# One order for the upper and lower passes in all four feed-forward halves, and another set of PSUM banks for their first block

## The chip, the cores and the metric

One core of a Trainium2 chip runs the whole program. The metric is the device time of one execution in microseconds; the median of the runs is given, and a profiled execution of its own shows where the time goes. TensorE (PE) multiplies, ScalarE (ACT) and VectorE (DVE) prepare its operands and read its results out of PSUM, SyncE (SP) issues the loads, and GpSimd (POOL) does little here.

## The reference

Two layers work on x of 256 tokens x 1024. What matters here are the two SwiGLU half steps of each layer, four in the program:

```
def swiglu(h, w_in, w_out):
    gate, up = jnp.split(h @ w_in, 2, axis=-1)
    return (jax.nn.silu(gate) * up) @ w_out

for i in range(DEPTH):                                    # DEPTH = 2, D_FF = 2816
    x = x + 0.5 * swiglu(rms_norm(x, norm_ffn1[i]), ffn1_w_in[i], ffn1_w_out[i])
    ...                                                   # attention, x = x + o @ w_o[i]
    x = x + 0.5 * swiglu(rms_norm(x, norm_ffn2[i]), ffn2_w_in[i], ffn2_w_out[i])
    ...                                                   # x = x + gate * (p[i] @ w_ple_proj[i])
```

## The kernel before

Every fp32 operand is split into an upper part and a lower part that PE takes as fp32r. For the weights, ACT writes the upper part `whi` (L236, L238) and DVE the lower part `wlo` (L243, L245), eight tiles ahead of PE at most. A product is upper x upper, upper x lower and lower x upper.

A half step (`ffn`) works on eleven blocks of 256 hidden columns. The **first block** has the tokens as its rows (`unit_cols`), one bank for each half of the tokens: 48 matmuls of 512 columns. Its result goes through Silu on ACT (L655) and a product on DVE (L661), and is turned by four PE transposes (`h_T`). In the first half step these two banks are of the kind `acc`; in the other three they are of the kind `mm`. The **other ten blocks** have the hidden columns as their rows (`columns`): four banks (two `mm`, one `tp`, one `op`) collect four chunks of weights. A chunk has eight pairs (k, n), n being the bank. A pair has an **upper pass** (`whi` against both parts of x, 512 columns) and a **lower pass** (`wlo` against the upper part of x, 256 columns). `COLUMN_GROUPS` says how many upper passes stand in a row ahead of their lower passes: 1 in the first half step, 2 in the second, 4 in the third, 8 in the fourth. After each column block come 24 or 18 matmuls of the output's product (`out_unit`, a **run** below) for an earlier block; they collect in the four `acc` banks. After the last block a run of 66 ends the half step.

The order on each engine is fixed when the program is built, by a model of the engines' times (`Pace`): helpers are put at the place at which the model finds their inputs ready and their bank free. The banks are four `acc`, two `mm`, one `tp` and one `op`; each kind is handed out in turn. At the end of a half step and of the attention the four `acc` banks are read into x by DVE (the attention's reading is L1130).

Of the kernel before, what the change touches and what calls it, by code (L numbers as in the profile page):

```python
# [108 lines left out]

COLUMN_GROUPS = (1, 2, 4, 8)


class Pace:
# [182 lines left out]
def encoder(ctx: ExitStack, tc, ins, out):  # L298
# [14 lines left out]
    pace = Pace()  # L313
# [6 lines left out]
    def can(kind):  # L320
        return slots[kind][turn[kind]] <= pace.now

    def take(kind, *tiles):
        assert can(kind), kind
        k = turn[kind]
        slots[kind][k] = 1e9
        turn[kind] = (k + 1) % len(slots[kind])
        for t in tiles:
            owner[id(t)] = (kind, k, t)
        return tiles[0] if len(tiles) == 1 else tiles  # L330
# [6 lines left out]
    def bank(kind):  # L337
        pool = {"acc": ps_acc, "mm": ps_mm}.get(kind, ps_tp)
        return take(kind, pool.tile([P, 512], F32, tag=kind, name=kind))
# [34 lines left out]
    def add_ffn(i, n, name):  # L374
        w_in, w_out = ins[name + "_in"][i], ins[name + "_out"][i]
        a, b = {}, {}
        for j in range(NFB):
            a[j] = add_cols(w_in[j], 2 * FB, n, i, uses=1 if j else 2)
            for m, kc, t in OUT_BEHIND.get(j, ()):
                if t == 0:  # L380
                    b[m, kc] = add_rows(w_out[2 * m + kc])
        for m, kc in OUT_LEFT:
            b[m, kc] = add_rows(w_out[2 * m + kc])
        return a, b

    plan = []
    for i in range(DEPTH):
        d = {"ffn1": add_ffn(i, 0, "ffn1")}
# [11 lines left out]
    def mm(ps, lhsT, rhs, start, stop, ready=0.0):  # L400
        nc.tensor.matmul(ps, lhsT=lhsT, rhs=rhs, start=start, stop=stop)  # L401
        pace.pe(0.0125 + rhs.shape[-1] / 2400, ready)
# [6 lines left out]
    def unit_cols(ps, a, t, ids, c, cw, kks=None):  # L409

        nk = 1024 // cw
        pace.until(lambda: all(a.cell[t][k].get("lo") for k in range(c * nk, c * nk + nk)))
        kks = kks or range(nk)
        wh, wl = W.get(ids[c])
        for kk in kks:
            k = c * nk + kk
            s = slice(kk * cw, (kk + 1) * cw)
            mm3(ps[:, :cw], a.hi[t][:, k, :], a.lo[t][:, k, :], wh[:, s], wl[:, s], k == 0, k == KD - 1,
                max(W.when[ids[c]], a.cell[t][k]["lo"]))
            if kk == nk - 1:  # L420
                W.used(ids[c])
            pace.check()
# [210 lines left out]
        pace.act(1500, pace.now)  # L633


    def ffn(a, ids, stage, first=False):

# [1 line left out]
        acc, hT, hs, made = [], {}, {}, {}  # L641
# [9 lines left out]
        def evac(t, ps, ts, done=None):  # L651
            pace.until(lambda: can("sq") and can("L") and a.has_r[t])
            s_t = scratch("sq")
            s = s_t[:, :FB]
            nc.scalar.activation(s, ps[:, :FB], AF.Silu, scale=a.r[t])  # L655
            t1 = pace.act(FB, max(done or pace.done(), a.has_r[t]), scale=True)
            if not hs:
                hs[0] = tile_L()

            def prod():  # L660
                nc.vector.tensor_tensor(out=hs[0][:, t, :], in0=ps[:, FB:], in1=s, op=ALU.mult)  # L661
                t2 = pace.dve(FB, t1)
                give(s_t)
                give(ps, t2)
                if ts:
                    with_bank("acc", t2 + 1.5, lambda: h_T(ts, t2))
            pace.at(t1, prod, "dve", 1)

        def first_evac(t, ps):
            if a.has_r[t]:  # L670
                evac(t, ps, [0, 1] if t else [], pace.now)
            else:
                pace.at(pace.now + 0.1, lambda: first_evac(t, ps))
# [34 lines left out]
        def columns(j):  # L708

            kinds = ("mm", "mm", "tp", "op")  # L710
            pace.until(lambda: all(max(slots[kind]) <= pace.now for kind in kinds))
            banks = [bank(kind) for kind in kinds]
            for c in range(4):
                ks = (2 * c, 2 * c + 1)
                pace.until(lambda: all(a.cell[t][k].get("lo") for t in range(2) for k in ks))
                wh, wl = W.get(ids_in[j][c])
                r = max(W.when[ids_in[j][c]], *(a.cell[t][k]["lo"] for t in range(2) for k in ks))
                every = [(k, n) for k in ks for n in range(4)]
                step = COLUMN_GROUPS[stage]
                for g in range(0, 8, step):  # L720
                    for lower in range(2):
                        for k, n in every[g:g + step]:
                            x2 = xhl[:, k, :, :].rearrange("p u q -> p (u q)")
                            o = slice(512 * (k % 2) + P * n, 512 * (k % 2) + P * (n + 1))
                            if lower:
                                mm(banks[n][:, S:], wl[:, o], x2[:, :S], False, k == KD - 1)
                            else:
                                mm(banks[n], wh[:, o], x2, k == 0, False, r)
                            pace.check()
                W.used(ids_in[j][c])  # L730
                pace.check()
            for kc in range(2):
                product(j, kc, banks[kc], banks[2 + kc])

        def product(j, kc, g_ps, u_ps):
            pace.until(lambda: can("sq") and "r" in has)
            gu = scratch("sq")
            g, u = gu[:, :S], gu[:, S:]
            p0 = pace.done()

            def gate():
                nc.scalar.copy(g, g_ps[:, :S])  # L742
                t1 = pace.act(S, p0)
                nc.scalar.copy(u, u_ps[:, :S])
                t2 = pace.act(S, p0)
                pace.at(t1, lambda: gate_sum(t1), "dve", 0)
                pace.at(t2, lambda: other_sum(t2), "dve", 1)

            def gate_sum(t1):
                nc.vector.tensor_tensor(out=g, in0=g_ps[:, S:], in1=g, op=ALU.add)  # L750
                give(g_ps, pace.dve(S, t1))
                nc.vector.tensor_tensor(out=g, in0=g, in1=rms_b, op=ALU.mult)
                t3 = pace.dve(S, has["r"])
                pace.at(t3, lambda: act(t3), "act", 1)

            def other_sum(t2):
                nc.vector.tensor_tensor(out=u, in0=u_ps[:, S:], in1=u, op=ALU.add)  # L757
                give(u_ps, pace.dve(S, t2))

            def act(t1):  # L760
                nc.scalar.activation(g, g, AF.Silu)
                t2 = pace.act(S, t1, sbuf=True)
                pace.at(t2, lambda: prod(t2), "dve", 1)

            def prod(t2):
                nc.vector.tensor_tensor(out=u, in0=u, in1=g, op=ALU.mult)
                t3 = pace.dve(S, t2)
                split(t3)

            def split(t3):  # L770
                if j not in hT and not can("pt"):
                    pace.at(pace.now + 0.1, lambda: split(t3))
                    return
                hh, hl = slot(j)
                made[j, kc] = parts(hh[:, kc, :], hl[:, kc, :], u, S, ready=t3, then=lambda end: give(gu))
            pace.at(p0, gate, "act", 1)
# [22 lines left out]
        ps = []  # L799
        pace.at(pace.now, lambda: spread(0))  # L800
        if first:
            ps = [bank("acc") for t in range(2)]
            for k in range(KD):
                for t in range(2):
                    unit_cols(ps[t], a, t, ids_in[0], k // 2, 512, [k % 2])
                    if k == KD - 1:
                        first_evac(t, ps[t])
        else:
            for t in range(2):
                pace.until(lambda: can("mm"))  # L810
                ps.append(bank("mm"))
                for c in range(4):
                    unit_cols(ps[t], a, t, ids_in[0], c, 512)
                evac(t, ps[t], [0, 1] if t else [])
        for j in range(1, NFB):
            columns(j)
            for unit in OUT_BEHIND[j]:
                out_unit(*unit)
# [391 lines left out]
    a = first_acts()  # L1210
# [2 lines left out]
    table(AF.Silu)  # L1213
    for i in range(DEPTH):
        d = plan[i]
        a = ffn(a, d["ffn1"], 2 * i, first=(i == 0))
        a, ple = mixers(i, a, d)
        a = ffn(a, d["ffn2"], 2 * i + 1)
        a = gate(a, d["gate"], ple, final=(i == DEPTH - 1))


# [14 lines left out]
```

## Time and profile before

| | us |
|---|---|
| median of 3 runs | 1037.63 |
| the runs | 1037.04 to 1039.37 |
| profiled execution | 1036.9 |
| its span on the core | 1035.1 |
| PE busy | 1021.1 (99%) |
| DVE busy | 767.5 (74%) |
| ACT busy | 687.1 (66%) |

The span is the time from the first to the last instruction of the program; the profiled execution's own time has 1.8 us around it. PE's records overlap: a matmul of 512 columns is shown with some 0.39 us, but the next starts some 0.23 us after it. So the pitch (start to start) is read, not the length. The four half steps lie at about 5 to 196, 311 to 498, 520 to 708 and 823 to 1009 us.

### The profile page before, as it was taken

What the parts mean: (1) busy time and instruction counts of PE and PEld (TensorE: products, weight loads), DVE (VectorE), ACT (ScalarE), POOL (GpSimd) and SP (SyncE); (2) the same over time, 40 slices, a digit from 0 to 9 for tenths busy, and PEclk for the clock granted to TensorE, in tenths of its full rate; (3) what the DMA queues carried; (4) which work ended last, traced back from release to release, by engine and by line L of the source; (5) the groups of instructions that cost most, each with busy time, mean ns of one, the idle gap of its engine ahead of it and who ended that gap; (6) DMA issues with size and microseconds to landing.
All of it is one profiled execution on the core that took longest, in us unless ns stands there. A gap on an engine that the chain in (4) does not pass through costs nothing.

```text
span 1035.1 us, 15614 instructions
## 1 busy us (share of the span) xinstructions
PE 1021.1 (99%) x5466; PEld 872.1 (84%) x5466; DVE 767.5 (74%) x1578; ACT 687.1 (66%) x1438; POOL 34.6 (3%) x38
## 2 busy tenths in 40 slices
PE   8999999999999999999999999999999999999998
PEld 7888888879887888888888888888888888888887
DVE  6686875888896757857887478578898876678575
ACT  8875754678886646746876467467779875467463
POOL 0000000120100000000000000001110000000000
PEclk9999999999999999999999999999999999999999
DMA  8664754455455546645664457444654466366361
GB/s 301 213 211 155 268 177 145 161 188 177 149 169 197 162 131 210 225 155 182 217 201 163 154 171 257 163 133 173 214 158 148 143 218 215 99 234 226 103 208 62
DMA packets 55911, 187.30 MB, mean 181 GB/s; under 512 B 6502, under 2 KB 10854, under 8 KB 55832
## 3 DMA queue, kind: packets, MB, share of 16 engines
q1 hardware_dynamic: 55832, 186.30, 54.3%
q8 instruction: 43, 0.70, 0.3%
q14 instruction: 36, 0.29, 0.1%
HBM read 185.19 MB, written 1.08 MB: 180 GB/s over the span
## 4 chain that ended last, share of the span: by engine, by line
PE 89%; DVE 5%; ACT 2%; DMA 2%; issue 1%; POOL 0%; SPq 0%; ACTq 0%
PE acc L401 34%; PE mm L401 28%; PE op L401 12%; PE tp L401 10%; PE tp L438 2%; DVE wlo L245 2%; DMA wraw<-in_ffn_in_dram 1%; DVE wlo L243 1%; DVE hss L862 1%; DMA wraw<-in_qkv_dram 1%; PE op L438 1%; ACT whi L238 1%; PE acc L438 0%; POOL hrs L866 0%; ACT kah L458 0%
## 5 line engine op out<-in xcount | busy, mean ns | idle before, releaser
L245 DVE SCALAR_TENSOR_TENSOR wlo<-wraw,gains,whi 128x512 fp32r<-128x512 f32 (+1 forms) x464 | 318.9, 738 | 54.5 <-ACT whi L238 52.9
L238 ACT ACTIVATE whi<-wraw,gains 128x512 fp32r<-128x512 f32 (+1 forms) x464 | 301.4, 707 | 70.0 <-DMA wraw<-in_ffn_in_dram 41.2
L401 PE MATMUL mm<-xhl,whi 128*128 128x512 f32 x640 | 211.7, 396 | 3.8 <-DVE L L661 3.5
L243 DVE TENSOR_TENSOR wlo<-wraw,whi 128x512 fp32r<-128x512 f32 x216 | 140.3, 686 | 29.8 <-ACT whi L236 24.5
L236 ACT CAST whi<-wraw 128x512 fp32r<-128x512 f32 x216 | 124.2, 617 | 56.5 <-PE op L401 29.3
L401 PE MATMUL mm<-xhl,wlo 128*128 128x256 f32 x640 | 140.5, 281 | 0.0
L401 PE MATMUL acc<-whi,pth 128*128 128x512 f32 x352 | 137.8, 392 | 0.0
L401 PE MATMUL acc<-whi,ptl 128*128 128x512 f32 x352 | 137.4, 390 | 0.0
L401 PE MATMUL acc<-wlo,pth 128*128 128x512 f32 x352 | 137.4, 390 | 0.0
L401 PEld LDWEIGHTS mm<-xhl,wlo 128*128 128x128 f32 x640 | 117.8, 189 | 17.0
L401 PE MATMUL tp<-xhl,whi 128*128 128x512 f32 x320 | 126.1, 394 | 0.2 <-DVE sq L757 0.2
L401 PE MATMUL op<-xhl,whi 128*128 128x512 f32 x320 | 126.3, 395 | 0.0
L401 PEld LDWEIGHTS mm<-xhl,whi 128*128 128x128 f32 x640 | 108.5, 189 | 19.3 <-DVE L L661 4.8
L750 DVE TENSOR_TENSOR sq<-mm,sq 128x256 f32<-128x256 f32 x80 | 33.7, 422 | 113.2 <-ACT sq L742 112.4
L401 PE MATMUL mm<-whi,xhl 128*128 128x512 f32 (+1 forms) x304 | 100.5, 391 | 0.0
L401 PE MATMUL tp<-xhl,wlo 128*128 128x256 f32 x320 | 89.7, 280 | 0.0
L401 PE MATMUL op<-xhl,wlo 128*128 128x256 f32 x320 | 89.4, 280 | 0.0
L742 ACT COPY sq<-mm 128x256 f32<-128x256 f32 x80 | 30.2, 377 | 88.2 <-PE mm L401 88.2
L401 PE MATMUL acc<-whi,xhl 128*128 128x512 f32 (+1 forms) x288 | 83.1, 363 | 1.0 <-ACT whi L238 1.0
L401 PEld LDWEIGHTS acc<-whi,ptl 128*128 128x128 f32 x352 | 66.1, 188 | 14.3
L401 PEld LDWEIGHTS acc<-whi,pth 128*128 128x128 f32 x352 | 66.1, 188 | 12.9
L401 PEld LDWEIGHTS acc<-wlo,pth 128*128 128x128 f32 x352 | 66.1, 188 | 12.4
(155 smaller groups left out, 1576.5 us busy)
## 6 DMA issues: line engine op xcount, KB each, us to landing
wraw<-in_ffn_in_dram SPq DMA_DIRECT2D x172, 512.0 KB, 4.5
wraw<-in_ffn_out_dram SPq DMA_DIRECT2D x88, 512.0 KB, 4.8
wraw<-in_qkv_dram SPq DMA_DIRECT2D x36, 512.0 KB, 3.5
wraw<-in_wo_dram SPq DMA_DIRECT2D x16, 512.0 KB, 3.5
wraw<-in_gate_dram SPq DMA_DIRECT2D x16, 512.0 KB, 4.5
bias<-bias_d SPq DMA_DIRECT2D x32, 192.0 KB, 4.0
wraw<-in_ffn_in_dram SPq DMA_DIRECT2D x8, 256.0 KB, 5.5
wraw<-in_ple_dram SPq DMA_DIRECT2D x4, 512.0 KB, 5.0
```

Source lines behind the costliest of these rows:

```text
L236: nc.scalar.copy(hi[:, a:b], raw[:, a:b])
L238: nc.scalar.activation(hi[:, a:b], raw[:, a:b], AF.Copy, scale=g)
L243: nc.vector.tensor_tensor(out=lo[:, a:b], in0=raw[:, a:b], in1=hi[:, a:b].bitcast(F32), op=ALU.subtract)
L245: nc.vector.scalar_tensor_tensor(out=lo[:, a:b], in0=raw[:, a:b], scalar=g, in1=hi[:, a:b].bitcast(F32), op0=ALU.mult, op1=ALU.subtract)
L401: nc.tensor.matmul(ps, lhsT=lhsT, rhs=rhs, start=start, stop=stop)
L438: nc.tensor.transpose(tp[:, n * P:(n + 1) * P], src, ident)
L742: nc.scalar.copy(g, g_ps[:, :S])
L750: nc.vector.tensor_tensor(out=g, in0=g_ps[:, S:], in1=g, op=ALU.add)
L862: nc.vector.tensor_reduce(out=ss[:, :nh], in_=sq[:, :w].rearrange("p (h d) -> p h d", d=HD), axis=AX.X, op=ALU.add)
```

## The change

```
-COLUMN_GROUPS = (1, 2, 4, 8)
+COLUMN_GROUP = 8
...
-    def ffn(a, ids, stage, first=False):
+    def ffn(a, ids, first=False):
...
-                step = COLUMN_GROUPS[stage]
+                step = COLUMN_GROUP
                 for g in range(0, 8, step):
                     for lower in range(2):
                         for k, n in every[g:g + step]:
...
         else:
             for t in range(2):
-                pace.until(lambda: can("mm"))
-                ps.append(bank("mm"))
+                pace.until(lambda: can("acc"))
+                ps.append(bank("acc"))
                 for c in range(4):
                     unit_cols(ps[t], a, t, ids_in[0], c, 512)
                 evac(t, ps[t], [0, 1] if t else [])
```

All half steps now have eight upper passes in a row and then eight lower ones, as the fourth had before. The two banks of the first block are `acc` in all four.

On PE, at the start of the first column block of the first half step (about 17.8 us), upper and lower passes alternated before:

```order
L401 MATMUL mm<-xhl,whi 128x512
L401 MATMUL mm<-xhl,wlo 128x256
L401 MATMUL mm<-xhl,whi 128x512
L401 MATMUL mm<-xhl,wlo 128x256
L401 MATMUL tp<-xhl,whi 128x512
L401 MATMUL tp<-xhl,wlo 128x256
L401 MATMUL op<-xhl,whi 128x512
L401 MATMUL op<-xhl,wlo 128x256
```

Now the block starts with:

```order
L401 MATMUL mm<-xhl,whi 128x512 x2
L401 MATMUL tp<-xhl,whi 128x512
L401 MATMUL op<-xhl,whi 128x512
L401 MATMUL mm<-xhl,whi 128x512 x2
L401 MATMUL tp<-xhl,whi 128x512
L401 MATMUL op<-xhl,whi 128x512
```

The fourth bank was first written by the seventh matmul; now the first four matmuls write all four banks.

On PE, at the end of the second half step's first block and the start of its first column block (about 321 us), this stood before:

```order
L401 MATMUL mm<-wlo,xhl 128x512
L401 MATMUL mm<-whi,xhl 128x512
L401 MATMUL mm<-xhl,whi 128x512 x2
L401 MATMUL mm<-xhl,wlo 128x256 x2
L401 MATMUL tp<-xhl,whi 128x512
L401 MATMUL op<-xhl,whi 128x512
L401 MATMUL tp<-xhl,wlo 128x256
L401 MATMUL op<-xhl,wlo 128x256
L401 MATMUL mm<-xhl,whi 128x512
L438 MATMUL acc<-ident,L 128x128 x4
```

This stands there now:

```order
L401 MATMUL acc<-wlo,xhl 128x512
L401 MATMUL acc<-whi,xhl 128x512
L401 MATMUL mm<-xhl,whi 128x512 x2
L401 MATMUL tp<-xhl,whi 128x512
L401 MATMUL op<-xhl,whi 128x512
L401 MATMUL mm<-xhl,whi 128x512 x2
L401 MATMUL tp<-xhl,whi 128x512
L401 MATMUL op<-xhl,whi 128x512
L401 MATMUL mm<-xhl,wlo 128x256 x2
L401 MATMUL tp<-xhl,wlo 128x256
L401 MATMUL op<-xhl,wlo 128x256
```

The matmuls of the first block write `acc` where they wrote `mm`, and so the two `mm` banks that the column block takes are no longer those that the first block has just filled. The four transposes of `h_T` (the last row of before) stand behind 20 passes of the column block, where they stood behind 9; in the third half step behind 16 instead of 9, in the fourth behind 17 instead of 7.

On ACT in the second half step, the split of the turned first block (L458, `pth`) stood behind three splits of weights:

```order
L655 ACTIVATE sq<-mm,r_3463 128x256
L238 ACTIVATE whi<-wraw,gains 128x512 x3
L458 CAST pth<-acc 128x512
L238 ACTIVATE whi<-wraw,gains 128x512 x4
```

Now it stands behind five:

```order
L655 ACTIVATE sq<-acc,r_3463 128x256
L238 ACTIVATE whi<-wraw,gains 128x512 x5
L458 CAST pth<-acc 128x512
L238 ACTIVATE whi<-wraw,gains 128x512 x2
```

DVE's lower parts move with it, and in the third half step both engines have one weight split more ahead of it. Nothing else changes its place on ACT, DVE, POOL or SP, and on PE everything outside the column passes and these transposes keeps its order.

## Rows read from the trace of the kernel before

**Rows 1.** The page: the clock that TensorE was granted, in 40 slices of the span.

```profile
PEclk9999999999999999999999999999999999999999
```

**Rows 2.** Waits of PE: engine, line, releaser: us in total, times, longest.

```profile
PE mm L401 <- DVE L L661: 3.5, 3, 1.6
```

**Rows 3.** Timeline of PE, second half step: start, length, instruction, [idle before <-releaser].

```profile
321.29 0.39 PE L401 MATMUL mm<-whi,xhl 128*128 128x512 f32 x1
321.51 0.39 PE L401 MATMUL mm<-xhl,whi 128*128 128x512 f32 x1
323.52 0.50 PE L401 MATMUL mm<-xhl,whi 128*128 128x512 f32 x1 [1.62 <-DVE L L661]
323.85 0.40 PE L401 MATMUL mm<-xhl,wlo 128*128 128x256 f32 x2
```

**Rows 4.** The same view at the same place of the third and fourth half steps.

```profile
531.73 0.39 PE L401 MATMUL mm<-xhl,whi 128*128 128x512 f32 x1
533.00 0.50 PE L401 MATMUL mm<-xhl,whi 128*128 128x512 f32 x1 [0.88 <-DVE L L661]
...
833.02 0.39 PE L401 MATMUL mm<-xhl,whi 128*128 128x512 f32 x1
834.43 0.50 PE L401 MATMUL mm<-xhl,whi 128*128 128x512 f32 x1 [1.01 <-DVE L L661]
```

**Rows 5.** Chain that ended last: start, length, piece. Runs of the output's product.

```profile
81.12 5.47 PE acc L401 x24
...
179.13 10.95 PE acc L401 x48
...
335.15 5.45 PE acc L401 x24
...
480.35 10.90 PE acc L401 x48
...
544.67 5.49 PE acc L401 x24
...
690.77 10.94 PE acc L401 x48
...
846.09 5.47 PE acc L401 x24
...
943.05 5.47 PE acc L401 x24
...
991.53 8.64 PE acc L401 x38
```

**Rows 6.** Timeline of PE, first half step (two rows), then fourth (two rows).

```profile
119.70 0.40 PE L401 MATMUL op<-xhl,whi 128*128 128x512 f32 x1
...
121.11 0.40 PE L401 MATMUL op<-xhl,whi 128*128 128x512 f32 x1
...
934.50 0.63 PE L401 MATMUL mm<-xhl,whi 128*128 128x512 f32 x2
...
937.30 0.63 PE L401 MATMUL mm<-xhl,whi 128*128 128x512 f32 x2
```

**Rows 7.** Timeline of PE, first half step, the fourth column block's start.

```profile
68.86 0.50 PE L401 MATMUL mm<-xhl,whi 128*128 128x512 f32 x1
...
70.90 0.40 PE L401 MATMUL op<-xhl,whi 128*128 128x512 f32 x1
```

**Rows 8.** Chain that ended last, ahead of that block.

```profile
59.53 5.34 DMA wraw<-in_ffn_in_dram
...
65.73 2.75 DVE wlo L245 x4
```

**Rows 9.** Timelines of DVE and PE, second half step: last bank read, next column block.

```profile
371.64 0.41 DVE L757 TENSOR_TENSOR sq<-op,sq 128x256 f32<-128x256 f32 x1
...
372.25 0.62 PE L401 MATMUL mm<-xhl,whi 128*128 128x512 f32 x2
```

**Rows 10.** Timeline of DVE ahead of the second half step: the reading of `acc`.

```profile
309.89 1.28 DVE L1130 TENSOR_TENSOR x_sb<-acc,x_sb 128x512 f32<-128x512 f32 x2
```

More of the change, by code (lines that the diff above doesn't have):

```diff
@@ L108 @@
 OUT_LEFT = [(j, kc) for j in range(NFB - 2, NFB) for kc in range(2)]
-COLUMN_GROUPS = (1, 2, 4, 8)
+COLUMN_GROUP = 8
 class Pace:
@@ L633, in table, with ffn @@
         pace.act(1500, pace.now)
-    def ffn(a, ids, stage, first=False):
+    def ffn(a, ids, first=False):
         ids_in, ids_out = ids
@@ L718, in columns @@
                 every = [(k, n) for k in ks for n in range(4)]
-                step = COLUMN_GROUPS[stage]
+                step = COLUMN_GROUP
                 for g in range(0, 8, step):
@@ L809, in ffn @@
             for t in range(2):
-                pace.until(lambda: can("mm"))
-                ps.append(bank("mm"))
+                pace.until(lambda: can("acc"))
+                ps.append(bank("acc"))
                 for c in range(4):
@@ L1215, in encoder @@
         d = plan[i]
-        a = ffn(a, d["ffn1"], 2 * i, first=(i == 0))
+        a = ffn(a, d["ffn1"], first=(i == 0))
         a, ple = mixers(i, a, d)
-        a = ffn(a, d["ffn2"], 2 * i + 1)
+        a = ffn(a, d["ffn2"])
         a = gate(a, d["gate"], ple, final=(i == DEPTH - 1))
```

## The prediction

> **What bounds the kernel now.** I read the page first, then the waits of PE, then the chain that ended last, and last the timelines around the places that the change touches. The page has PE busy in every slice, and the clock granted is full in all 40 [rows 1], which is the 2.4 GHz level: there is no clock to win or lose here, and time comes only from PE's pitch or from gaps between its matmuls. The list of waits has one entry over 3 us, three waits for the product of the first block [rows 2]. The timeline shows one of them: an upper pass into the first mm bank starts at 321.51, the next one, into the second mm bank, at 323.52, when DVE has read that bank out (L661) [rows 3]. The chain of the four half steps is nearly all PE in its alternation of column blocks and runs, so a pitch that is shorter there shortens the program.
>
> **The first block into acc.** The second mm bank holds the second half of the tokens, whose last matmul ends the first block. Silu and the product must pass before the column block can write there. With acc the two mm banks are long free. The usual pitch of a 512-column matmul is 0.22 to 0.23 us [rows 3], so the gaps lose 2.01 - 0.23 = 1.78 us in the second half step, 1.27 - 0.23 = 1.04 in the third and 1.41 - 0.23 = 1.18 in the fourth [rows 3, 4]: 4.0 in all. The matmul after such a gap has a pitch of 0.33 instead of 0.23 [rows 3]; I take that 0.1 as part of the gap, three times, 0.3 more. The first half step gives nothing here, since it used acc already. Sum: -4.3 us.
>
> Does the wait come back at the acc banks? The ring hands the first block the two banks that were read first at the end of the stage before, and even the last reading ends at 309.89 + 1.28 = 311.2 us [rows 10], ten us ahead of the place where PE stalls. The next who takes an acc bank after the block is the little turn of the norms, and then h_T; all four banks are needed together only by the run at 335 us. So I cost this at nothing. It would cost at most what the wait gave, if the release came as late as L661 does now. What stood in the shadow of the gap is h_T: its transposes need the product that ended the gap, and they now stand 20 passes (3.7 us at the fourth half step's pace, by 0.35 us a pair) into a block that starts some 1.8 us earlier. That is still some 1.9 us after the product. Its result is wanted by the run a whole column block later, so the two weight splits that ACT now does ahead of it are covered too.
>
> **Eight upper and eight lower passes.** The kernel before holds the four orders side by side, each with the same blocks, so their price is read from the chain. Runs start at fixed points of a period (column block plus run), and the spans between the same runs can be compared [rows 5]:
> - second half step (groups of two), nine periods: 480.35 - 335.15 = 145.20 us
> - third (four): 690.77 - 544.67 = 146.10 us
> - fourth (eight): 991.53 - 846.09 = 145.44 us
> - first (one), its last six periods: 179.13 - 81.12 = 98.01 us, against the six like ones of the fourth: 943.05 - 846.09 = 96.96 us
>
> With groups of eight everywhere, the second half step loses 0.24 us and the third gains 0.66; the first column block, outside these spans, adds a ninth part, so +0.27 and -0.73. The first half step gains 1.05 us in those six periods. The single pairs agree: 1.41 us for four alternating pairs, 0.3525 each, against 2.80 for eight grouped ones, 0.350 each [rows 6], the rest being at the seams of blocks and runs. So grouping is not better the longer it is: two is the cheapest of the four.
>
> The first four column blocks of the first half step are another matter. The fourth does not start when PE is ready: it waits for its banks, mm at 68.86, and the last, op, is first written at 70.90 [rows 7]. Behind that stands a chain which is not PE's: weights that land at 59.53 + 5.34 = 64.87 us, and DVE's four lower parts up to 68.5 [rows 8], ahead of the reads that free the banks. What PE gains in the second and third block is lost in this wait; only the first period's gain goes into that chain, (98.01 - 96.96)/6 = 0.18 us. And the new order is worse in this one place: when op is free, three alternating pairs were done before, 3 x 0.3525 = 1.06 us of the block's work; now it is three upper passes, 3 x 0.23 = 0.69, since the fourth must write op. That is 0.37 lost; the shorter block gives back some 0.14, and the chain 0.18. With the slower matmul after each of the waits I take +0.1 us for the start and -1.05 for the rest: -0.95. Its bounds: -0.6 if the wait grows by the whole 0.37, -1.3 if it is not felt.
>
> **Sum.** -4.3 (gaps) - 0.95 + 0.27 - 0.73 (order) = -5.7 us. The profiled execution had 1036.9 us, so it would have 1031.2; the median of the runs lies 0.7 above that execution, so I forecast a median of 1031.9 us, 0.55% less.
>
> **Rivals.**
> - The order is worth nothing. Half steps differ by where they stand, not by their order: for it speaks that two passes in a row are better than eight, which no simple price for a change of operand would give; against it, that the pairs themselves differ inside a block [rows 6]. Then only the gaps go, -4.3 us, and the median is 1033.3. The Trainium skill ("TensorE: Matmul & The Clock Gate", section "Back-to-back issue gap") gives each warm matmul N/2.4 + 2.5 ns, whatever its neighbour, an estimate of 325 ns a pair in any order; the pairs here take 350 to 353 and so do not go by it alone.
> - The wait moves. PE comes 1 to 1.8 us earlier to the first column block, and something that was hidden by the gap is late next, say weights or the turned block. Nothing on PE's list of waits but the start of the program and the heads' norms points there. If all of the gaps came back as such waits, only the order's -1.4 us would stay: 1036.2.
> - It gets slower, by the banks. A column block needs op at its fourth matmul, 3 x 0.23 = 0.69 us after its start, where alternation left 1.06. In the tightest blocks, after a run of 18, the read of op ends at 371.64 + 0.41 = 372.05, and the column block starts at 372.25 [rows 9]: 0.9 us to spare. The price: in twelve such blocks, whatever the read is later than that. To lose the 5.7 us that the rest gives, the reads would have to end 0.9 + 5.7/12 = 1.4 us later than now. The fourth half step has this order already and no such wait. To end above the time before by 0.3%, 1040.7, it takes 1.6 us.
>
> **How the numbers follow.** My forecast has a chance of 0.84, the inert order 0.08, the moved wait 0.05, the banks 0.03. The forecast's own range comes from the start of the first half step (-0.6 to -1.3), the 0.3 after the gaps, and the spread between a single execution and a median (the runs shown go from 1037.04 to 1039.37): 1030.6 to 1033.2. To leave no more than 2 in 10 out it is enough to take in the inert order too: 1030.5 to 1033.7. A measurement tells some 0.2%, 2 us, from no change: the forecast and the inert order are beyond that, the moved wait is mostly within, the banks above. Faster 0.92, same 0.05, slower 0.03.
>
> **What would show it.** Right: the wait on L661 is gone from PE's list, in each of the three later half steps the second upper pass of the first column block follows the first by 0.23 us, and all four half steps have the fourth's periods, nine of them 145.4 us. The fourth column block of the first half step starts near 68.7 us and still waits for tp and op. Wrong: PE waits for an acc bank in the first block, for h_T or for a weight in the first column block, or for op in the blocks after runs of 18; or a half step keeps a pace of its own in spite of the order.

## The result and the profile after

The changed kernel takes 1032.71 us (median of 4 runs, 1032.03 to 1033.57), against 1038.04 for the kernel before beside it: a ratio of 0.9948, 95% interval 0.9931 to 0.9966. Forecast were 0.9945 and 1031.9 us, in a range of 1030.5 to 1033.7. The profiled execution took 1033.04 us, with a span of 1031.2, 3.9 us less than before; forecast were 5.7. The medians differ by 5.3 us, so the sum is right to a tenth there; the two traces differ by a third less than forecast. One term shows why: the first half step of this trace is not shorter but longer. The same kernel, run again later (1031.52 us, 0.9945; span 1030.2), gave a second trace; both are read below.

The waits of PE in the changed kernel (us in total, times, longest), in answer to [rows 2], the four at the head of the list:

```profile
PE tp L438 <- DVE qn L884: 2.2, 4, 1.0
PE acc L513 <- POOL ident masks.py:199: 1.4, 1, 1.4
PE op L401 <- DVE sq L527: 0.9, 1, 0.9
PE acc L401 <- ACT whi L238: 0.5, 1, 0.5
```

The three waits for L661, at the head of the list before, are gone, and no wait for an acc bank has come. A new one stands in third place: PE waits once, for 0.9 us, until DVE has read (L527) the op bank which the setup of the bias table had taken. The timeline of PE at the second half step's first column block answers to [rows 3]:

```profile
321.58 0.39 PE L401 MATMUL acc<-whi,xhl 128*128 128x512 f32 x1
321.81 0.62 PE L401 MATMUL mm<-xhl,whi 128*128 128x512 f32 x2
322.26 0.39 PE L401 MATMUL tp<-xhl,whi 128*128 128x512 f32 x1
322.49 0.39 PE L401 MATMUL op<-xhl,whi 128*128 128x512 f32 x1
```

Four upper passes start 0.22 to 0.23 us apart where a gap of 2.01 us was. The runs in the chain that ended last answer to [rows 5]:

```profile
82.58 5.47 PE acc L401 x24
...
179.54 10.92 PE acc L401 x48
...
333.58 5.47 PE acc L401 x24
...
479.02 10.92 PE acc L401 x48
...
542.21 5.47 PE acc L401 x24
...
687.67 10.92 PE acc L401 x48
...
841.79 5.47 PE acc L401 x24
...
987.84 10.92 PE acc L401 x48
```

The six periods of the first half step take 179.54 - 82.58 = 96.96 us, to the hundredth what the fourth took before. The nine of the second take 145.44, of the third 145.46 (before 145.20 and 146.10), and of the fourth 146.05, 0.6 more than before: in one block there ACT had waited for a load, and its copies out of the banks were late.

```profile
924.68 0.62 ACT L236 CAST whi<-wraw 128x512 fp32r<-128x512 f32 x1 [1.92 <-DMA wraw<-in_ffn_out_dram]
```

The second trace has the fourth half step without that wait, and one of 0.3 us in the third. The rest of what is lost lies ahead of 82 us. The timeline of PE in the second column block of the first half step:

```profile
35.12 1.03 PE L524 MATMUL op<-qn,rb 34*16 34x512 f32 x2
36.08 0.72 PE L401 MATMUL mm<-xhl,whi 128*128 128x512 f32 x2
36.65 0.40 PE L401 MATMUL tp<-xhl,whi 128*128 128x512 f32 x1
37.93 0.50 PE L401 MATMUL op<-xhl,whi 128*128 128x512 f32 x1 [0.89 <-DVE sq L527]
38.26 0.85 PE L401 MATMUL mm<-xhl,whi 128*128 128x512 f32 x2
38.92 0.63 PE L401 MATMUL tp<-xhl,whi 128*128 128x512 f32 x1
39.34 0.63 PE L401 MATMUL op<-xhl,whi 128*128 128x512 f32 x1
```

The block's fourth upper pass waits 1.28 us behind the third, and behind that the pitch is not 0.23 but 0.42. Busy times by stretch (length, PE, PEld, DVE, ACT, POOL, then the granted clock, DMA's share, GB/s) say why:

```profile
36.00:38.00 2.00, 1.11 (x5) 0.56 (x4) 2.00 (x8) 2.00 (x5) 0.00 (x0) 1.00 0.02 6
38.00:43.00 5.00, 5.00 (x19) 4.35 (x20) 4.45 (x8) 3.04 (x7) 0.00 (x0) 0.66 0.65 173
43.00:50.00 7.00, 7.00 (x43) 6.20 (x43) 1.23 (x2) 6.94 (x12) 0.00 (x0) 1.00 0.67 258
```

Behind the wait the clock stood at its lower level, 1.2 GHz, for some 3.4 us: 0.66 is the mean over 5 us, and at the lower level it would be 0.50. The block lasts 13.98 us: 1.05 of the 2.83 over 11.15 are the wait, about 1.7 the clock.

DVE came late to that bank. Its read began 0.10 us behind the block's start in the kernel before, and 1.12 us behind it here (DVE's timelines, before and then after):

```profile
36.32 0.68 DVE L527 COPY sq<-op 16x512 f32<-16x512 f32 x1
```

```profile
37.20 0.67 DVE L527 COPY sq<-op 16x512 f32<-16x512 f32 x1
```

It was late because ACT, whose work DVE's own stands behind, had waited longer for a load than before (ACT's timelines, before and then after):

```profile
29.41 1.95 ACT L238 ACTIVATE whi<-wraw,gains 128x512 fp32r<-128x512 f32 x3 [0.92 <-DMA wraw<-in_ffn_in_dram]
```

```profile
30.25 2.18 ACT L238 ACTIVATE whi<-wraw,gains 128x512 fp32r<-128x512 f32 x3 [1.68 <-DMA wraw<-in_ffn_in_dram]
```

The chain that ended last goes from a load that lands at 31.68 us through ACT's splits and copies and DVE's reads to L527. In the other traces with setup at this place ACT's wait lies between 0.88 and 1.36 us.

### The profile page after: what moved, and what is told of

It is laid out like the page before. It is cut to its first block, busy times and chain, and to the rows that moved or that the text cites. A ratio compares the mean times of both kernels' runs of the same rounds, so it can differ in the third digit from the quotient of the medians.

```text
span 1031.2 us, 15613 instructions
## 1 busy us (share of the span) xinstructions
PE 1020.5 (99%) x5466; PEld 875.0 (85%) x5466; DVE 766.7 (74%) x1578; ACT 687.5 (67%) x1438; POOL 34.6 (3%) x38
## 4 chain that ended last, share of the span: by engine, by line
PE 86%; DVE 6%; DMA 4%; ACT 3%; issue 1%; POOL 0%; SPq 0%; ACTq 0%; DVEq 0%
PE acc L401 35%; PE mm L401 25%; PE op L401 12%; PE tp L401 10%; DMA wraw<-in_ffn_in_dram 2%; PE tp L438 2%; DVE wlo L245 2%; DVE hss L862 1%; ACT whi L238 1%; DMA wraw<-in_qkv_dram 1%; PE op L438 1%; DVE wlo L243 1%; DMA wraw<-in_ffn_out_dram 1%; POOL hrs L866 0%; PE acc L438 0%
## 5 line engine op out<-in xcount | busy, mean ns | idle before, releaser
L401 PE MATMUL mm<-xhl,whi 128*128 128x512 f32 x640 | 200.4, 394 | 0.0
L401 PE MATMUL mm<-xhl,wlo 128*128 128x256 f32 x640 | 128.3, 282 | 0.0
L401 PEld LDWEIGHTS mm<-xhl,whi 128*128 128x128 f32 x640 | 112.6, 190 | 17.0 <-issue 0.9
L401 PEld LDWEIGHTS mm<-xhl,wlo 128*128 128x128 f32 x640 | 110.5, 191 | 12.6
L401 PE MATMUL acc<-whi,xhl 128*128 128x512 f32 (+1 forms) x384 | 114.8, 371 | 0.5 <-ACT whi L238 0.5
L401 PEld LDWEIGHTS acc<-whi,xhl 128*128 128x128 f32 x384 | 70.4, 188 | 12.4 <-ACT whi L238 0.7
```

## The experiments

The ratio is that to the kernel before beside each. "First half step" below means the time on PE from its first column block's start to the start of its last run: 161.1 us before, 161.7 in the changed kernel's first trace and 160.6 in its second.

**The order alone**, on the kernel before.

```
-COLUMN_GROUPS = (1, 2, 4, 8)
+COLUMN_GROUPS = (8, 8, 8, 8)
```

> Groups of eight everywhere, the first block left on its mm banks. Theory (the order sets the pitch, the gaps are a matter of the banks): every column block lasts 11.15 us and every run of 24 5.47 us in all four half steps, and the three gaps of 1.8, 1.0 and 1.2 us stay. Without the trouble of the first half step's second column block the time is 1.4 us under the kernel before; with the wait and the slow clock that the changed kernel's trace shows there, about the same as before, within 0.7 us. Rival (half steps differ by their place): column blocks keep 11.29, 11.14, 11.20, 11.15.

Measured: 1036.77 us (11 runs), 0.9994 (0.9985 to 1.0002). Column blocks last 11.146 us and runs 5.468 in all four half steps, and PE's list still has 3.5 us for L661. So the order sets the pitch, wherever it stands. By the interval its whole is worth 0.0 to 0.15%, so the time alone does not show that it is worth anything; 1.4 us would be 0.13%. The first half step took 160.4 us, 0.7 less than before, and had no slow clock. Some 0.8 us were lost between this half step's last run and the second half step, where the order is not touched; why is open.

**The banks alone**, on the kernel before.

```
-                pace.until(lambda: can("mm"))
-                ps.append(bank("mm"))
+                pace.until(lambda: can("acc"))
+                ps.append(bank("acc"))
```

> Groups of 1, 2, 4, 8 as before, the first block on acc in all four half steps. Theory: the three gaps go, 4.3 us under the kernel before (0.9959), the pitches stay as before. The first half step has no wait for op at its second column block beyond what the kernel before has, since alternation writes op last. Rival (the wait moves to an acc bank or to a weight): less than 2 us gained.

Measured: 1033.52 us, 0.9961 (0.9947 to 0.9974), a hundredth of a per cent or two from the forecast 0.9959. No wait for L661 is left. The banks are the larger part of the change, about three quarters.

**Setup put off**, on the changed kernel.

```
-    pace.at(30.0, lambda: when(setup, "sq", "op"))
+    pace.at(120.0, lambda: when(setup, "sq", "op"))
```

> The changed kernel, with the small setup work (the bias table's matmul on the op bank, its copy by DVE, and its store) put off from a planned 30 us to 120 us. Theory (the second column block waits for op because DVE's copy out of setup's bank is late, and the clock falls behind that wait): no wait of over 0.3 us and full clock from 35 to 50 us; the fourth column block still waits for its banks, behind loads, so that 1 to 2 of the 2.8 us come back: 1030.7 to 1031.7 in place of 1032.7. Rival (late weights hold this stretch whatever setup does): the same time as the changed kernel.

Measured: 1033.45 us, 0.9956 (0.9943 to 0.9968): no gain, the time that the rival gave. The trace is of the longest of the five runs, 1034.47 us; the others took 1031.48 to 1033.75, and how much of what follows they had is not shown. The second column block is now 11.146 us with no wait, so setup's bank was the cause there. But the fourth block waits more, and here the clock falls. Timeline of PE, and the busy times of the stretch:

```profile
67.15 0.39 PE L401 MATMUL acc<-whi,ptl 128*128 128x512 f32 x1
68.29 0.50 PE L401 MATMUL mm<-xhl,whi 128*128 128x512 f32 x1 [0.75 <-DVE sq L750]
69.08 0.50 PE L401 MATMUL mm<-xhl,whi 128*128 128x512 f32 x1 [0.29 <-DVE sq L750]
69.88 0.50 PE L401 MATMUL tp<-xhl,whi 128*128 128x512 f32 x1 [0.29 <-DVE sq L757]
```

```profile
68.00:74.00 6.00, 5.13 (x17) 3.92 (x18) 5.70 (x14) 4.34 (x11) 0.00 (x0) 0.72 0.59 200
```

In this trace, what was won in the second block was lost in the fourth: 0.9 us in the run's last gap, 2.9 in the block.

**Groups of two**, on the changed kernel.

```
-COLUMN_GROUP = 8
+COLUMN_GROUP = 2
```

> The changed kernel with groups of two in all four half steps in place of eight. Theory (the order sets the pitch wherever it stands): column blocks of 11.14 and runs of 5.45 us in all four half steps, 0.026 us a period, 1.0 us under the changed kernel, and as much as 1 us more at the start of the first half step, where op is first written by the sixth matmul instead of the fourth. Rival (the second half step's pace is its place): no better than the changed kernel.

Measured: 1030.90 us, 0.9935 (0.9922 to 0.9947). Column blocks last 11.137 and most runs 5.450 us in all four half steps. That is 0.03 us a period, as between the half steps of the kernel before; beside the changed kernel's 0.9948 and 0.9945 the time alone would not settle it. The first half step, 160.5 us, still loses 2.2 us at the fourth block.

**The zero fills put off**, on the changed kernel. ACT fills the attention's pads with zeros (L548), 14 fills with little between them, from about 43 to 53 us.

```
-    pace.at(40.0, zero_pads)
+    pace.at(100.0, zero_pads)
```

> The changed kernel with ScalarE's zero fills of the attention's pads (8 us of L548 at about 43 to 52 us) planned at 100 us instead of 40. Theory (those fills hold ScalarE's weight splits back, so that the loads and the reads that free the banks are late for the fourth column block): the wait at the fourth column block (0.5 us of 11.63 in the changed kernel's trace) goes, the one at the second stays, since it comes ahead of the fills: 0.5 to 1 us less, about 1032. Rival (the loads themselves are too slow in the first 70 us): no change.

Measured: 1032.05 us, 0.9947 (0.9934 to 0.9961). The fourth column block lasts 11.146 us, without a wait. But the ninth, some 36 us behind the fills' new place (103 to 113 us), has 13.09:

```profile
149.15 0.47 PE L401 MATMUL mm<-xhl,whi 128*128 128x512 f32 x1
150.61 0.47 PE L401 MATMUL mm<-xhl,whi 128*128 128x512 f32 x1 [0.98 <-DVE sq L750]
151.40 0.47 PE L401 MATMUL tp<-xhl,whi 128*128 128x512 f32 x1 [0.33 <-DVE sq L757]
```

The wait has moved, neither theory's result. That the time is near the theory's 1032 says nothing: the changed kernel beside it took 1031.52 us.

**Both put off** (fills to 100, setup to 130 us), with groups of eight, and then with groups of two.

> The changed kernel with both the zero fills (100 us) and the setup work (130 us) later. Theory: neither the second nor the fourth column block waits or falls to the slow clock; of the 3.8 us that the fourth lost with the setup alone moved (0.9 in the run ahead of it, 2.9 in the block) nearly all come back: 1029.5 to 1031. Rival (the loads are too slow): as with the setup alone moved, 1033.4.

Measured: 1031.91 us, 0.9948 (0.9935 to 0.9960), not the 1029.5 to 1031 of the theory. The fourth block is clean, but the third has 12.00 us, and the one behind setup's new place waits 1.05 us for the op bank, again on L527. Why the third block waits is open; PE came to it some 1.4 us earlier, from the first block's start, than with the fills alone put off.

> As the kernel with both moved, but with groups of two. Theory: the 2.2 us that the fourth column block and the run ahead of it lost in the kernel of twos come back, less up to 0.5 us around setup's new place: 1028.5 to 1029.5. Rival (the loads are too slow): 1030.9 as with groups of two alone.

Measured: 1030.89 us, 0.9939 (0.9926 to 0.9951): as with groups of two alone, which was the rival's figure. In these runs, moving this work as a block moves the waits.

**The changed kernel again**, unedited.

> The changed kernel once more, beside the others and with a trace of its own. Theory: 0.9948 of the kernel before, within 0.0010; every column block but the second and fourth of the first half step at 11.15 us. [...]

Measured: 1031.52 us, 0.9945 (0.9932 to 0.9957). The second block lasts 11.56 us, not 13.98; the clock stays full. The fourth does the waiting instead (PE's timeline):

```profile
68.55 0.39 PE L401 MATMUL acc<-whi,ptl 128*128 128x512 f32 x1
69.34 0.49 PE L401 MATMUL mm<-xhl,whi 128*128 128x512 f32 x1 [0.41 <-DVE sq L750]
70.14 0.49 PE L401 MATMUL mm<-xhl,whi 128*128 128x512 f32 x1 [0.30 <-DVE sq L750]
70.93 0.49 PE L401 MATMUL tp<-xhl,whi 128*128 128x512 f32 x1 [0.30 <-DVE sq L757]
```

The block lasts 12.51 us and the run ahead of it 4.68 instead of 4.11. So the slow clock is not in every execution, and a loss at the start of the program is in both traces.

**The fills one at a time**, with groups of two and of eight.

```
+        late = iter(range(0, 200, 8))
         for dst in pads:
-            pace.at(pace.now, lambda dst=dst: zero(dst), "act", 9)
+            pace.at(pace.now + next(late), lambda dst=dst: zero(dst), "act", 9)
...
-    pace.at(40.0, zero_pads)
+    pace.at(75.0, zero_pads)
```

The eight fills of the k pads get the same `next(late)`.

> Groups of two with the first block on acc, and the fourteen zero fills of ScalarE one at a time, planned every 8 us from 75 us on, in place of all in a row at 40 us. Theory (the wait at the fourth column block comes from the fills in a row, and went with them wherever they were put in a row): no column block of the first half step waits for a bank by more than 0.3 us except perhaps the second, behind setup; 2.2 us less than groups of two alone: 1028.7, 0.9915 of the kernel before. Rival (the loads of the first 70 us are too slow, and any order of ScalarE's work pays for them somewhere): 1030.9.

Measured: 1027.32 us (4 runs, 1026.92 to 1028.32), 0.9895 (0.9882 to 0.9909), the fastest of the study, 1% under the kernel before. The whole list of PE's waits:

```profile
PE tp L438 <- DVE qn L885: 1.5, 3, 1.0
PE acc L513 <- POOL ident masks.py:199: 1.4, 1, 1.4
PE acc L401 <- DVE wlo L245: 0.6, 2, 0.3
PE tp L438 <- DVE ri L1002: 0.4, 2, 0.2
PE acc L401 <- ACT whi L238: 0.2, 1, 0.2
PE tp L438 <- DVE x_sb L1131: 0.2, 1, 0.2
```

No column block's wait for a bank is on the list any more; only the second block, behind setup, is still 0.27 us longer than the others. The first half step takes 158.4 us, 2.2 less than with twos alone, as the theory said. Another 1.1 us came at a place that no theory named: the stretch from its last run to the second half step's first column block is 141.6 instead of 142.7 us, with one wait for the transposed heads (`qn`) less; why is open.

> The same spread of the fills, with groups of eight as in the changed kernel. Theory: the 1.9 us at the fourth column block of the changed kernel's second trace come back: 1029.8 in place of 1031.7; and against the kernel of twos with the same spread it is 1.0 us longer, 0.26 us in each half step and no more, since no wait is left in which the order of the banks matters. Rival: no better than the changed kernel.

Measured: 1029.18 us (5 runs, 1028.79 to 1029.60), 0.9912 (0.9899 to 0.9926), beyond the interval of the changed kernel in its later runs (0.9932 to 0.9957). So both rivals, that the loads are too slow whatever ACT's order and that the spread is worth nothing, have fallen. The first half step takes 158.6 us. Twos and eights were on the same chip here and the runs do not overlap; the spans, 1025.8 and 1027.0 us, differ by 1.2, of which 1.0 were expected.

## Why the prediction was right, and where it was not

**The ratio** came nearer than the terms did, and that is in part luck. The profiled execution of the kernel before lay 1.1 us under its median, that of the changed kernel 0.3 above; the forecast had taken 0.7 under for both. So of the 1.8 us that the traces fall short of the 5.7, the medians show 0.4. The second trace, 4.9 us shorter, falls short by 0.8.

**The gaps** were sized rightly. The first column block of the second, third and fourth half steps went from 13.48, 12.78 and 12.90 us to 11.61, 11.59 and 11.60: 1.87, 1.19 and 1.30 us less, 4.4 together. Forecast were 4.3, and in the third half step 0.05 of the order's. The banks alone gave the same. The rival that the wait moves has fallen in these three places: nothing is late next there. The transposes of h_T stand at 325.51 us in the changed kernel, without a wait.

**The order** was priced rightly as a pitch. 0.27 us lost in the second half step and 0.73 won in the third were forecast; the nine periods gave 0.24 and 0.64. The rival that the order is inert has fallen: with eights and with twos all four half steps take the same period, which the place does not change. And two is cheaper than eight also where eight stood. The formula that the prediction quotes with that rival is given in that section of the Trainium skill for an isolated matmul, so it never said that pairs in a stream must cost the same.

**The start of the first half step** was mis-sized: -0.95 us was forecast, bounds -0.6 and -1.3. The traces gave +0.5 (with the slow clock), -0.5 (the second trace) and -0.7 (order alone). The step that failed is the one that took +0.1 us for what happens ahead of the fifth block: by the same traces it was +1.6, +0.6 and +0.3. For the later six periods the 1.05 us came exactly. In the second trace the run and the fourth block lose 1.9 us to waits against 1.1 before. I had seen that all four banks are now wanted in the first four passes, but only at the fourth block. At the second block the op bank comes from setup, and DVE's read of it (L527) stands behind the first product and weights that were late from the start; by alternation PE came to op 1.06 us into the block, now after 0.69, and the three passes are all the work there is to wait with.

The order explains only the smaller part of the first trace's wait there. In the traces of order alone and of the fills put off, where the read begins as soon behind the block's start as before, the second block is 0.3 us too long; in the first trace the read ended 1.79 us into the block, and alternation would have waited for it too, by an estimate of 1.79 - 1.06 = 0.7 us. The rest came from the late load of that execution and from the clock.

**What held the fourth block** was not the loads as such, as I had it when I wrote of a chain that is not PE's. The zero fills in a row on ACT belong to it, and the chain of the kernel before, which [rows 8] shows only from 59.53 us on, runs through them:

```profile
44.86 1.04 ACT kah L548
45.91 1.05 ACT kah L548
48.03 1.05 ACT kal L548
```

Put off, the wait at the fourth block went, and another came behind them; one at a time (and from 75 instead of 100 us on), none was left. That the wait at 150 us with the fills at 103 to 113 is their doing is argued from these two, not followed step by step. Setup's share is shown at its old and new place.

**The rival of the banks**, too late a read in the later blocks, came true at one block of a trace at most, and behind runs of 24, not of 18: by 0.6 us in the first trace's fourth half step, where PE waited for tp, by 0.3 us in the second trace's third, and by 0.8 us with setup put off. It costs little and not in every execution.

## What to carry to other kernels

When one kernel holds several variants of an inner order side by side, its own trace prices them to a hundredth of a microsecond; read the seams between blocks too. An order that writes its accumulators in quick succession needs all of them free at the start: mind each place where a bank comes from someone else than the last block. A stretch that waited on several engines' queues gave back little for a faster PE; here it paid to spread low-priority work over the queue, one piece at a time, rather than to put it off in one lump.

## What was not expected of the hardware

The pitch of a matmul depends on its neighbours: in groups of eight, an upper pass (512 columns) takes 227 ns behind five or more others, but 228 to 236 in the first five places behind lower ones; a lower pass (256 columns) takes 113 ns behind an upper one and 120 behind lower ones. Groups of two are best of the four tried; what makes it so is open.

A short cluster of gaps can cost more than itself, but need not. The clock fell to its lower level in the changed kernel's first trace, after two small matmuls (weights of 34 rows x 16 columns, 0.96 us together), three upper passes and a pitch of 1.28 us; and with setup put off, after pitches of 1.14, 0.80 and 0.80 in a row. It did not fall after the single gap of 2.01 us of the kernel before [rows 3], after three pitches of 0.79 in the second trace, or after pitches of 1.46 and 0.79 with the fills put off. And with both put off it stayed full (1.00 from 134 to 140 us) behind the same small matmuls, the same three passes and the same pitch of 1.28 us (PE's timeline):

```profile
134.77 0.40 PE L401 MATMUL tp<-xhl,whi 128*128 128x512 f32 x1
136.05 0.50 PE L401 MATMUL op<-xhl,whi 128*128 128x512 f32 x1 [0.89 <-DVE sq L527]
```

So what decides it is open. At the lower level upper passes took 427 and lower ones 214 ns, for some 3.4 us, which cost about 1.7 us. The Trainium skill ("TensorE: Matmul & The Clock Gate", "Part 1: The HAM clock gate") has the clock depend on how busy the engine has been of late. The traces agree in so far as it fell only behind waits (0.66 granted from 38 to 43 us); they do not show more than that.
